# Stick-breaking attention in fixed turns, with odd blocks of tokens reversed and the running total in the last key's row

## The chip, the cores and the metric

One Trainium2 chip, one core of it. The metric is the device time of one execution in microseconds, median over runs. The core has a matrix engine (PE, TensorE), a vector engine (DVE, VectorE), a scalar engine (ACT, ScalarE), a general engine (POOL, GpSimd) and queues for transfers (SP). Each engine works through its own list of instructions in order; between engines, semaphores say when an operand is there or a buffer is free.

## The reference

Two decoder layers over 512 tokens of width 2048 in float32. The first is sparse attention with an indexer and a top-k; the second, which the change is about, is stick-breaking attention over keys and values that are computed once. Each layer ends with a gated output product, a layer norm and a gated per-layer embedding.

```python
def mixer_b(x, w_in, w_o, k, v):
    q, gate = jnp.split(x @ w_in, [WIDTH_B], axis=-1)      # 16 heads of 128, 4 key heads
    def block_fn(args):                                    # 128 queries at a time
        z = jnp.einsum('bqngd,bsnd->bngqs', qg, k).astype(jnp.float32) * (HEAD_DIM ** -0.5)
        strict = key_pos[None, :] < t[:, None]
        log_om = jnp.where(strict, -jax.nn.softplus(z), 0.0)
        suffix = lax.cumsum(log_om, axis=log_om.ndim - 1, reverse=True) - log_om
        a = jnp.where(strict, jnp.exp(jax.nn.log_sigmoid(z) + suffix), 0.0)
        o = jnp.einsum('bngqs,bsnd->bqngd', a.astype(v.dtype), v)
    return (o * jax.nn.silu(gate)) @ w_o
```

The weight of key s for query t is sigmoid(z) at s times the product of (1 - sigmoid(z)) over all keys between s and t. In logarithms that is z - (softplus(z) summed over the keys from s to t), so keys are worked through from the latest to the earliest and a total is carried from one block of keys to the next.

## The kernel before

Activations lie transposed, features in partitions and tokens along the free axis. All products are float32 made of three products of high and low parts: `split` (L131) copies the high part on ScalarE and subtracts on VectorE, `mm3` (L135) issues the three matmuls of 128x512. TensorE's order is exactly the order of the program text; the other engines' instructions are put in order by a scheduler, except for those that are held in program order (`paced`, L325, and `keep_in_program_order`).

The second layer's attention goes over four groups `g` of four heads, each with one key head. A group is worked together with the product for its gate: `gemm_w` (L289, and `gate_first`, L1213, for group 0) yields 64 steps, each of three matmuls, into four banks; every fourth step needs a new block of weights, which is split by one ScalarE and one VectorE instruction. `pumped` (L339) also does one piece of background work a step from the list `bg`: scaled and split queries of the next group (`split_scaled`, L1207), split keys, and in group 0 the restored halves of the layer's input (`restore`, L1147).

`sticks` (L1238) works the ten pairs of a query block i and a key block kb, `units` (L1240), in an order that alternates between query blocks. Four heads lie side by side, so each unit is 128 keys in partitions by 512. A unit has three parts:

- `logits` (L1245): three matmuls of keys and queries into a bank `z` (bank 7 for unit 0, then 4 and 5 in turn). On the diagonal (kb == i) VectorE adds the mask `gone`. ScalarE computes Abs, Exp and Ln; VectorE makes softplus out of them (L1258). Then comes bookkeeping in the first key's row, with instructions on one partition (L1259 to L1272): where a total is carried in, row 0 of `z` is replaced by the logarithm of sigmoid and row 0 of softplus by the total. At last VectorE splits softplus into `sh` and `sl`.
- `weights` (L1278): two matmuls with a triangle of -1 (`tri`, or `tri0` with a full first row, L1234) add the negative sums over the keys to `z` (L1282). VectorE takes the new total from row 0 (`y`, L1284); ScalarE computes Exp, and `split` makes high and low parts of the weights.
- `values` (L1292): three matmuls of values and weights into bank 6 or 7; after the last key block ScalarE copies the output into `F`.

The loop at L1300 issues `logits` of unit s, `weights` of s-1, `values` of s-2, for s from 0 to 11. `interleave` (L57) spreads the gate steps evenly between these parts: 64 - 18 over 28 parts in group 0 (L1343), 52 over 33 in the others after a lead of 8 (L1341), so some 1.6 gate steps behind each part. None of the instructions of `sticks` on ScalarE and VectorE is held in program order. After a group, four Silu and four multiplications apply the gate, and `log_exp` (L1222) loads the table of Exp and Ln again.

Of the kernel before, what the change touches and what calls it, by code (L numbers as in the profile page):

```python
# [10 lines left out]
F32 = mybir.dt.float32  # L11
# [7 lines left out]
T = 512  # L19
# [58 lines left out]
def trunk_kernel(  # L78
# [20 lines left out]
    class Paced:  # L99


        def __init__(self, engine):
            self.engine_ = engine
# [24 lines left out]
    def bank(i, name="ps"):  # L128
        return psum.tile([128, 512], F32, name=name, tag=f"bank{i}")

    def split(hi, lo, src, eng=dve):  # L131
        act.activation(hi, src, AF.Copy)
        eng.tensor_tensor(lo, src, hi.bitcast(F32), ALU.subtract)

    def mm3(out, a, b, start, stop):  # L135
        pe.matmul(out, a[0], b[0], start=start, stop=False)  # L136
        pe.matmul(out, a[0], b[1], start=False, stop=False)  # L137
        pe.matmul(out, a[1], b[0], start=False, stop=stop)  # L138
# [577 lines left out]
    def index_scores():  # L716
        for i in range(1, 4):
            w = 128 * (i + 1)
            for h in range(16):
                ps = spare("isc", 0)  # L720
                st = stacks[h][:, (i - 1) * 128 : i * 128]
                pe.matmul(ps[:, :w], st, B1[:, :w], start=True, stop=False)
                pe.matmul(ps[:, :w], st, B2[:, :w], start=False, stop=True)
                rl = ip.tile([128, T], F32, name="rl", tag="rl", bufs=3)
                act.activation(rl[:, :w], ps[:, :w], AF.Relu)
                wcol = iws[:, i - 1, h : h + 1]
                if h == 0:
# [5 lines left out]
            pool.affine_select(out=diag, in_=diag, pattern=[[-1, 128]], compare_op=ALU.is_ge, fill=FILL, base=0, channel_multiplier=1)  # L733
# [473 lines left out]
    def split_scaled(g, i):  # L1207
        qh, ql = (q.rearrange("p (h q) -> p h q", h=4) for q in Q[i])
        src = F[g][:, :, i * 128 : (i + 1) * 128]
        act.activation(qh, src, AF.Copy, scale=HSCALE)  # L1210
        dve.scalar_tensor_tensor(ql, src, HSCALE, qh.bitcast(F32), ALU.mult, ALU.subtract)
# [11 lines left out]
        tc.keep_in_program_order(act.preload_act_table_set("natural_log_exp_and_others"))  # L1223

    def work():
        return px.tile([128, 512], F32, name="wk", tag="wk", bufs=5)


    gone = px.tile([128, 128], F32, name="gone")
    pool.memset(gone, 0.0)  # L1230
    pool.affine_select(out=gone, in_=gone, pattern=[[1, 128]], compare_op=ALU.is_gt, fill=MASK, base=0, channel_multiplier=-1)
# [6 lines left out]
    def sticks(g, Q):  # L1238

        units = [(3, 3), (2, 2), (3, 2), (2, 1), (3, 1), (2, 0), (3, 0), (1, 1), (0, 0), (1, 0)]  # L1240
        total = {}
        state = {}
        out = {}

        def logits(u):  # L1245
            i, kb = units[u]
            z = bank(4 + u % 2 if u else 7, "z")
            ks = slice(kb * 128, (kb + 1) * 128)
            mm3(z, [k[:, ks] for k in K[g]], Q[i], True, True)
            e = work()  # L1250
            sp = work()
            if kb == i:
                v = z.rearrange("p (h q) -> p h q", h=4)
                dve.tensor_tensor(v, v, gone.unsqueeze(1).broadcast_to([128, 4, 128]), ALU.add)
            act.activation(e, z, AF.Abs)
            act.activation(e, e, AF.Exp, scale=-1.0)
            act.activation(e, e, AF.Ln, bias=1.0)
            dve.scalar_tensor_tensor(sp, z, 0.0, e, ALU.max, ALU.add)  # L1258
            first = None  # L1259
            if kb:  # L1260
                first = px.tile([1, 512], F32, name="y", tag="y", bufs=3)
            if kb == i:
                if kb:
                    dve.tensor_copy(first, z[0:1])
            else:

                if kb:
                    dve.scalar_tensor_tensor(first, z[0:1], 0.0, e[0:1], ALU.min, ALU.subtract)
                    dve.tensor_copy(z[0:1], first)
                else:  # L1270
                    dve.scalar_tensor_tensor(z[0:1], z[0:1], 0.0, e[0:1], ALU.min, ALU.subtract)
                dve.tensor_copy(sp[0:1], total.pop(i))  # L1272
            parts = tuple(px.tile([128, 512], F32R, name=f"s{s}", tag=f"s{s}", bufs=3) for s in "hl")
            dve.tensor_copy(parts[0], sp)
            dve.tensor_tensor(parts[1], sp, parts[0].bitcast(F32), ALU.subtract)
            state[u] = z, parts, first

        def weights(u):  # L1278
            i, kb = units[u]
            z, parts, first = state[u]  # L1280
            for n, p in enumerate(parts):
                pe.matmul(z, tri if kb == i else tri0, p, start=False, stop=n == 1, skip_group_check=True)  # L1282
            if kb:
                dve.tensor_tensor(first, first, z[0:1], ALU.subtract)  # L1284
                total[i] = first
            a = work()
            act.activation(a, z, AF.Exp)
            parts = A[u % 2]
            split(*parts, a)
            state[u] = parts  # L1290

        def values(u):  # L1292
            i, kb = units[u]
            if kb == i:
                out[i] = bank(6 if i in (0, 3) else 7, "o")
            mm3(out[i], [v[:, g * 128 : (g + 1) * 128] for v in V[kb]], state.pop(u), kb == i, kb == 0)
            if kb == 0:
                act.activation(F[g][:, :, i * 128 : (i + 1) * 128], out[i].rearrange("p (h q) -> p h q", h=4), AF.Copy)

        for s in range(12):  # L1300

            done = [i for n, (i, kb) in enumerate(units) if kb == 0 and s == max(n + 3, 0 if g else 8) and n < 9]
            if g < 3:
                bg.extend(lambda i=i: split_scaled(g + 1, i) for i in done)
            for fn, u in ((logits, s), (weights, s - 1), (values, s - 2)):
                if 0 <= u < 10:
                    fn(u)
                    yield
                if g and s == 1 and fn == logits:
                    for _ in range(4):  # L1310
                        yield

    log_exp()

# [5 lines left out]
    banks = mm_banks("g")  # L1320
    chunk = gate_first(banks)
    gemm = pumped(chunk)
    first = sticks(0, Q)
    for n in (9, 1):
        steps(gemm, n)
        steps(first, 1)
    bg.extend(lambda i=i: split_scaled(0, i) for i in (1, 0))
    steps(gemm, 8)
    gemm = pumped(chunk, 2)
# [1 line left out]
    for g in range(4):  # L1331
        if g:
            log_exp()
            banks = mm_banks("g")
            gemm = pumped(gemm_w(items, plain, banks))
        if 0 < g < 3:
            bg.append(lambda g=g: split_keys(g + 1))
        if g:
            sums = sticks(g, Q)
            steps(sums, 1)  # L1340
            interleave(sums, 29 + 4, gemm, 52, lead=8)  # L1341
        else:
# [60 lines left out]
```

## Time and profile before

| what | value |
|---|---|
| median of 3 runs | 1885.15 us (1885.1 to 1885.21) |
| profiled execution | 1884.75 us |
| its span, first to last instruction | 1882.9 us |
| granted TensorE clock | 1.000 |

Names: `z` is a bank of logits, `sh` and `sl` the parts of softplus, `y` the row with the total, `wk` any working tile, `wh` and `wl` the parts of a block of weights, `g` the banks of the gate, `o` those of an output (and of the next projection), `f` the tiles `F`, `c` the tiles with keys, values, queries and weights in parts. In the lists of groups, a row has the line, engine, operation, output and input, shape and count, then busy time, mean of one in nanoseconds, and the idle time in front of it with what ended it. A row of the timeline has the start, the duration, the engine and the instruction, and in brackets the idle time ahead of it. All of line 111 are ScalarE and VectorE instructions that were recorded through the class `Paced`. A row of waits says who waited for whom, microseconds in total, how often, and the longest.

### The profile page before, as it was taken

To read this page: it belongs to the slowest core of one execution; us is meant where nothing else is said; L and a number is where in the kernel's file an instruction comes from. 1 tells how busy PE (TensorE), PEld (TensorE's weight loads), DVE (VectorE), ACT (ScalarE), POOL (GpSimd) and SP (SyncE) were. 2 spreads that over 40 slices of the span, in tenths; PEclk is the share of its full clock that TensorE was granted. 3 is DMA by queue.
4 is the path that set the end of the run, shared out by engine and by line. 5 is a ranking of instruction groups with operands and counts; after the bars stand their busy time and mean duration, and the time that the engine had idled before them with its cause. 6 is when DMAs were issued, how large, how long until landed. Compare 5 with 4: busy or idle time off the path is not lost.

```text
span 1882.9 us, 24826 instructions
## 1 busy us (share of the span) xinstructions
PE 1860.2 (99%) x9181; PEld 1574.2 (84%) x9181; DVE 1247.3 (66%) x2444; ACT 923.5 (49%) x1672; POOL 3.9 (0%) x16
## 2 busy tenths in 40 slices
PE   9999999999999999999999999999999999999998
PEld 8898888888888888888888999977777788888887
DVE  5768678567565455675377888887887745567534
ACT  3546423455554432474245444467677643246422
POOL 0000000000000000000000000000000000000000
PEclk9999999999999999999999999999999999999999
DMA  6442333312222532433343333322121153242333
GB/s 196 127 124 62 96 101 90 101 56 68 72 65 66 180 99 77 125 101 113 105 144 110 105 100 109 104 78 89 56 68 57 56 190 95 79 129 91 123 101 112
DMA packets 111179, 189.21 MB, mean 100 GB/s; under 512 B 8529, under 2 KB 29009, under 8 KB 111057
## 3 DMA queue, kind: packets, MB, share of 16 engines
q1 hardware_dynamic: 111056, 187.62, 32.7%
q8 instruction: 72, 1.18, 0.3%
q14 instruction: 51, 0.41, 0.1%
HBM read 179.21 MB, written 8.39 MB: 100 GB/s over the span
## 4 chain that ended last, share of the span: by engine, by line
PE 93%; DVE 3%; ACT 2%; issue 1%; DMA 0%; SPq 0%; DVEq 0%; ACTq 0%
PE g L136 11%; PE g L137 11%; PE g L138 11%; PE o L137 7%; PE o L136 7%; PE o L138 7%; PE m L136 4%; PE m L138 4%; PE m L137 4%; PE q L137 3%; PE q L138 3%; PE q L136 3%; PE k L137 2%; PE k L138 2%; PE k L136 2%; ACT wk L111 1%
## 5 line engine op out<-in xcount | busy, mean ns | idle before, releaser
L111 ACT ACTIVATE wh<-raw 128x512 fp32r<-128x512 f32 (+3 forms) x685 | 397.8, 582 | 703.7 <-PE g L137 235.2
L111 DVE TENSOR_TENSOR wl<-raw,wh 128x512 fp32r<-128x512 f32 (+3 forms) x685 | 430.3, 629 | 460.4 <-ACT wh L111 443.0
L136 PE MATMUL g<-xh,wh 128*128 128x512 f32 x1024 | 403.9, 394 | 0.0
L138 PE MATMUL g<-xh,wl 128*128 128x512 f32 x1024 | 399.5, 390 | 0.0
L137 PE MATMUL g<-xl,wh 128*128 128x512 f32 x1024 | 399.5, 390 | 0.0
L138 PEld LDWEIGHTS g<-xh,wl 128*128 128x128 f32 x1024 | 192.2, 188 | 41.2
L136 PEld LDWEIGHTS g<-xh,wh 128*128 128x128 f32 x1024 | 192.4, 188 | 37.6 <-ACT wk L111 0.8
L137 PEld LDWEIGHTS g<-xl,wh 128*128 128x128 f32 x1024 | 192.5, 188 | 37.2
L138 PE MATMUL o<-xh,wl 128*128 128x512 f32 x512 | 199.2, 389 | 0.0
L136 PE MATMUL o<-xh,wh 128*128 128x512 f32 x512 | 199.2, 389 | 0.0
L137 PE MATMUL o<-xl,wh 128*128 128x512 f32 x512 | 199.2, 389 | 0.0
L138 PEld LDWEIGHTS o<-xh,wl 128*128 128x128 f32 x512 | 96.1, 188 | 20.2
L136 PEld LDWEIGHTS o<-xh,wh 128*128 128x128 f32 x512 | 96.1, 188 | 19.9
L137 PEld LDWEIGHTS o<-xl,wh 128*128 128x128 f32 x512 | 96.1, 188 | 19.8
L136 PE MATMUL q<-xh,wh 128*128 128x512 f32 x256 | 99.6, 389 | 0.0
L137 PE MATMUL q<-xl,wh 128*128 128x512 f32 x256 | 99.6, 389 | 0.0
L138 PE MATMUL q<-xh,wl 128*128 128x512 f32 x256 | 99.6, 389 | 0.0
L111 ACT ACTIVATE wk<-z 128x512 f32<-128x512 f32 x80 | 47.4, 594 | 58.5 <-DVE z L111 24.2
L111 ACT ACTIVATE sh<-st 128x512 fp32r<-128x512 f32 x80 | 49.7, 624 | 44.4 <-DVE st L111 44.3
L111 DVE TENSOR_TENSOR sl<-st,sh 128x512 fp32r<-128x512 f32 x80 | 55.2, 691 | 13.9 <-ACT sh L111 13.9
L111 DVE TENSOR_TENSOR xl<-f,xh 128x512 fp32r<-128x512 f32 x80 | 54.3, 686 | 12.6 <-ACT f L111 12.3
L136 PEld LDWEIGHTS q<-xh,wh 128*128 128x128 f32 x256 | 48.0, 188 | 10.1
(284 smaller groups left out, 3327.0 us busy)
## 6 DMA issues: line engine op xcount, KB each, us to landing
raw<-w_in_a SPq DMA_DIRECT2D x95, 512.0 KB, 3.7
raw<-w_in_b SPq DMA_DIRECT2D x64, 512.0 KB, 3.8
raw<-w_ple_gate SPq DMA_DIRECT2D x52, 512.0 KB, 3.7
raw<-w_o_a SPq DMA_DIRECT2D x24, 512.0 KB, 3.8
raw<-w_o_b SPq DMA_DIRECT2D x24, 512.0 KB, 3.8
raw<-w_kv_b SPq DMA_DIRECT2D x16, 512.0 KB, 3.8
raw<-w_ple_gate SPq DMA_DIRECT2D x24, 256.0 KB, 2.9
f<-xT SPq DMA_DIRECT2D x4, 1024.0 KB, 6.3
```

The source lines that it names most:

```text
L111: ins = method(*args, **kw)
L136: pe.matmul(out, a[0], b[0], start=start, stop=False)
L137: pe.matmul(out, a[0], b[1], start=False, stop=False)
L138: pe.matmul(out, a[1], b[0], start=False, stop=stop)
```

## The change

- Odd query and key blocks (1 and 3) hold their 128 tokens in descending order. The host reorders the columns of x, of the embeddings and of the positions, and the rows of the result. The masks of the diagonal blocks are flipped for odd blocks, and a second triangle, `down`, serves odd key blocks.
- With that the total that is carried from one key block to the next lies in the last key's row: partition 0 for even key blocks, partition 127 for odd ones (instructions there work on the 32 rows from 96, with a column of the identity as factor so that only row 127 counts). The total is added to that row of softplus ahead of its split, so row 0 of `z` is no longer replaced. A copy of that row of `z` is taken on ScalarE ahead of the sums, and VectorE subtracts the new row from it afterwards.
- The splitting of softplus becomes a part of its own, `parts`. In `weights`, Exp is issued ahead of the subtraction for the total.
- `Sticks.turn` fixes the order: `logits` of s, gate steps, `values` of s-2, gate steps, `weights` of s-1 and `parts` of s, gate steps. The gate steps are 1, 1 and 3 in an ordinary turn (2 at the end of odd turns in group 0). Units 0 and 1 begin ahead of the turns; in groups 1 to 3, 11 gate steps follow them.
- All of these parts are called through `paced`, so their ScalarE and VectorE instructions are held in program order. The gate's weight splits and the Silu part are not.
- Buffers: `wk` 6 for 5, parts of softplus 2 for 3.

```diff
-    tri0 = px.tile([128, 128], F32R, name="tri0")
-    dve.tensor_copy(tri0, tri.bitcast(F32))
-    dve.tensor_copy(tri0[0:1], neg[0:1].bitcast(F32))
+    down = px.tile([128, 128], F32R, name="down")
+    gone = [px.tile([128, 128], F32, name=f"gone{n}") for n in range(2)]
...
+    for m, up in zip(gone, (1, -1)):
+        pool.memset(m, 0.0)
+        pool.affine_select(out=m, in_=m, pattern=[[up, 128]], compare_op=ALU.is_gt, fill=MASK, base=0, channel_multiplier=-up)
...
             act.activation(e, e, AF.Ln, bias=1.0)
             dve.scalar_tensor_tensor(sp, z, 0.0, e, ALU.max, ALU.add)
-            first = None
...
-                    dve.scalar_tensor_tensor(first, z[0:1], 0.0, e[0:1], ALU.min, ALU.subtract)
-                    dve.tensor_copy(z[0:1], first)
...
-                dve.tensor_copy(sp[0:1], total.pop(i))
...
+        def parts(self, u):
...
+            if kb < i:
+                total = self.total.pop(i)
+                if kb % 2:
+                    dve.tensor_tensor(sp[0:1], sp[0:1], total[0:1], ALU.add)
+                else:
+                    rows = slice(96, 128)
+                    dve.scalar_tensor_tensor(sp[rows], total[rows], ident[rows, 127:128], sp[rows], ALU.mult, ALU.add)
+            hi, lo = (px.tile([128, 512], F32R, name=f"s{s}", tag=f"s{s}", bufs=2) for s in "hl")
+            dve.tensor_copy(hi, sp)
+            dve.tensor_tensor(lo, sp, hi.bitcast(F32), ALU.subtract)
             if kb:
+                rows = slice(96, 128) if kb % 2 else slice(0, 1)
+                self.total[i, kb] = px.tile([128, 512], F32, name="t", tag="t", bufs=3)
+                act.activation(self.total[i, kb][rows], z[rows], AF.Copy)
...
+            for n, p in enumerate((hi, lo)):
+                pe.matmul(z, down if kb % 2 else tri, p, start=False, stop=n == 1, skip_group_check=True)
             a = work()
             act.activation(a, z, AF.Exp)
+            if kb:
+                rows = slice(96, 128) if kb % 2 else slice(0, 1)
+                total = self.total[i] = self.total.pop((i, kb))
+                dve.tensor_tensor(total[rows], total[rows], z[rows], ALU.subtract)
+            hi, lo = A[u % 2]
+            split(hi, lo, a)
...
+            pe.matmul(o, vh, hi, start=kb == i, stop=False)
+            pe.matmul(o, vl, hi, start=False, stop=False)
+            pe.matmul(o, vh, lo, start=False, stop=kb == 0)
...
+        def begin(self, u):
+            paced(self.logits, u)
+            if u == 0:
+                paced(self.parts, u)
+
+        def turn(self, s, gemm, gaps):
+            if 1 < s < 10:
+                paced(self.logits, s)
+            steps(gemm, gaps[0])
+            if s > 1:
+                paced(self.values, s - 2)
+            steps(gemm, gaps[1])
+            if s < 11:
+                paced(self.weights, s - 1)
+                if s < 10:
+                    paced(self.parts, s)
+            steps(gemm, gaps[2])
+            if self.g < 3 and s > 6:
+                bg.extend(lambda i=i: split_scaled(self.g + 1, i) for i in {8: (2,), 9: (3,), 11: (0,)}.get(s, ()))
...
-            interleave(sums, 29 + 4, gemm, 52, lead=8)
-        else:
-            interleave(first, 30 - 2, gemm, 64 - 18)
+        steps(gemm, 11 if g else 0)
+        for s in range(1, 12):
+            sticks.turn(s, gemm, (0 if s == 1 else 1, 1 if s > 1 else 0, 2 if s == 10 or not g and s % 2 else 3))
+        run(gemm)
...
-        "xT": lay(np.asarray(x)[0].T),
+        "xT": lay(np.asarray(x)[0][order].T),
```

More of the change, by code (lines that the diff above doesn't have):

```diff
@@ L1225, in work, with __init__, logits @@
     def work():
[L1226 to L1231, printed above, removed]
-    tri0 = px.tile([128, 128], F32R, name="tri0")
-    dve.tensor_copy(tri0, tri.bitcast(F32))
-    dve.tensor_copy(tri0[0:1], neg[0:1].bitcast(F32))
-    def sticks(g, Q):
-        units = [(3, 3), (2, 2), (3, 2), (2, 1), (3, 1), (2, 0), (3, 0), (1, 1), (0, 0), (1, 0)]
[L1241 to L1246, printed above, removed]
+        return px.tile([128, 512], F32, name="wk", tag="wk", bufs=6)
+    down = px.tile([128, 128], F32R, name="down")
+    gone = [px.tile([128, 128], F32, name=f"gone{n}") for n in range(2)]
+    ones = work()[:, :128]
+    pool.memset(ones, -1.0)
+    pool.affine_select(out=ones, in_=ones, pattern=[[1, 128]], compare_op=ALU.is_ge, fill=0.0, base=0, channel_multiplier=-1)
+    dve.tensor_copy(down, ones)
+    for m, up in zip(gone, (1, -1)):
+        pool.memset(m, 0.0)
+        pool.affine_select(out=m, in_=m, pattern=[[up, 128]], compare_op=ALU.is_gt, fill=MASK, base=0, channel_multiplier=-up)
+    class Sticks:
+        units = [(3, 3), (2, 2), (3, 2), (2, 1), (3, 1), (2, 0), (3, 0), (1, 1), (0, 0), (1, 0)]
+        def __init__(self, g):
+            self.g = g
+            self.total = {}
+            self.state = {}
+            self.out = {}
+        def logits(self, u):
+            i, kb = self.units[u]
             z = bank(4 + u % 2 if u else 7, "z")
             ks = slice(kb * 128, (kb + 1) * 128)
-            mm3(z, [k[:, ks] for k in K[g]], Q[i], True, True)
+            mm3(z, [k[:, ks] for k in K[self.g]], Q[i], True, True)
             e = work()
@@ L1253, in logits @@
                 v = z.rearrange("p (h q) -> p h q", h=4)
-                dve.tensor_tensor(v, v, gone.unsqueeze(1).broadcast_to([128, 4, 128]), ALU.add)
+                dve.tensor_tensor(v, v, gone[i % 2].unsqueeze(1).broadcast_to([128, 4, 128]), ALU.add)
             act.activation(e, z, AF.Abs)
@@ L1273, in logits @@
[L1273 to L1285, printed above, removed]
+            self.state[u] = z, sp
@@ L1286, in weights @@
+        def weights(self, u):
+            i, kb = self.units[u]
+            z, hi, lo = self.state[u]
+            for n, p in enumerate((hi, lo)):
+                pe.matmul(z, down if kb % 2 else tri, p, start=False, stop=n == 1, skip_group_check=True)
             a = work()
             act.activation(a, z, AF.Exp)
[L1288 to L1293, printed above, removed]
-            if kb == i:
-                out[i] = bank(6 if i in (0, 3) else 7, "o")
-            mm3(out[i], [v[:, g * 128 : (g + 1) * 128] for v in V[kb]], state.pop(u), kb == i, kb == 0)
-            if kb == 0:
-                act.activation(F[g][:, :, i * 128 : (i + 1) * 128], out[i].rearrange("p (h q) -> p h q", h=4), AF.Copy)
@@ L1300, in sticks @@
[L1300 to L1311, printed above, removed]
+            if kb:
+                rows = slice(96, 128) if kb % 2 else slice(0, 1)
+                total = self.total[i] = self.total.pop((i, kb))
+                dve.tensor_tensor(total[rows], total[rows], z[rows], ALU.subtract)
@@ new lines, in weights, with values @@
+            hi, lo = A[u % 2]
+            split(hi, lo, a)
+            self.state[u] = hi, lo
+        def values(self, u):
+            i, kb = self.units[u]
+            if kb == i:
+                self.out[i] = bank(6 if i in (0, 3) else 7, "o")
+            o = self.out[i]
+            hi, lo = self.state.pop(u)
+            vh, vl = (v[:, self.g * 128 : (self.g + 1) * 128] for v in V[kb])
+            pe.matmul(o, vh, hi, start=kb == i, stop=False)
+            pe.matmul(o, vl, hi, start=False, stop=False)
+            pe.matmul(o, vh, lo, start=False, stop=kb == 0)
+            if kb == 0:
+                act.activation(F[self.g][:, :, i * 128 : (i + 1) * 128], o.rearrange("p (h q) -> p h q", h=4), AF.Copy)
@@ L1322, in trunk_kernel @@
     gemm = pumped(chunk)
[L1323 to L1326, printed above, removed]
+    sticks = Sticks(0)
+    steps(gemm, 9)
+    sticks.begin(0)
+    steps(gemm, 1)
+    sticks.begin(1)
     bg.extend(lambda i=i: split_scaled(0, i) for i in (1, 0))
@@ L1379 @@
     ln = np.stack([np.asarray(ln_g), np.asarray(ln_b)]).reshape(2, 2, NK, 128)
+    order = np.arange(T).reshape(4, 128)
+    order[1::2] = order[1::2, ::-1].copy()
+    order = order.ravel()
+    lay = np.ascontiguousarray
+    ln = np.stack([np.asarray(ln_g), np.asarray(ln_b)]).reshape(2, 2, NK, 128)
     ins = {
-        "xT": lay(np.asarray(x)[0].T),
-        "pT": lay(np.asarray(p)[:, 0].transpose(0, 2, 1)),
-        "pos": lay(np.asarray(positions)),
+        "xT": lay(np.asarray(x)[0][order].T),
+        "pT": lay(np.asarray(p)[:, 0][:, order].transpose(0, 2, 1)),
+        "pos": lay(np.asarray(positions)[:, order]),
         "rope_c": rope,
@@ L1401 @@
     r = _run(nc, [ins], core_ids=[0])
-    return lay(np.asarray(r.results[0]["out_0_dram"]).T)[None]
+    return lay(np.asarray(r.results[0]["out_0_dram"]).T[order])[None]
```

20 lines of the change are left out of this document (8 added, 12 removed).

## The prediction

> **What bounds the kernel now.** I read the page first, then who makes TensorE wait, then the stretch with the stick-breaking layer row by row.
>
> ```profile
> span 1882.9 us, 24826 instructions
> PE 1860.2 (99%) x9181; PEld 1574.2 (84%) x9181; DVE 1247.3 (66%) x2444; ACT 923.5 (49%) x1672; POOL 3.9 (0%) x16
> PE 93%; DVE 3%; ACT 2%; issue 1%; DMA 0%; SPq 0%; DVEq 0%; ACTq 0%
> ```
>
> TensorE sets the time almost everywhere; only what makes it wait can be gained or lost. The list of TensorE's waits has nearly everything in one place, the banks `z` of the stick-breaking layer:
>
> ```profile
> PE z L1282 <- DVE sl L111: 7.1, 13, 1.3
> PE z L136 <- ACT wk L111: 4.5, 6, 1.0
> PE z L1282 <- DVE sh L111: 3.1, 7, 0.6
> ...
> PE o L137 <- DVE c L111: 1.2, 1, 1.2
> ```
>
> Line 1282 is the sum over the keys (`weights`), line 136 the first product of `logits`, line 137 a product of `values`. These microseconds undercount, because a matmul counts as busy for its 0.39 us although the next starts sooner. From the timeline of TensorE:
>
> ```profile
> 1342.77 0.39 PE L138 MATMUL o<-c,c 128*128 128x512 f32 x1
> ...
> 1345.94 0.47 PE L1282 MATMUL z<-sl,tri 128*128 128x512 f32 x1
> ...
> 1361.46 0.39 PE L138 MATMUL g<-xh,wl 128*128 128x512 f32 x1
> 1362.49 0.50 PE L1282 MATMUL z<-sh,tri 128*128 128x512 f32 x1 [0.64 <-DVE sh L111]
> 1363.22 0.50 PE L1282 MATMUL z<-sl,tri 128*128 128x512 f32 x1 [0.22 <-DVE sl L111]
> 1363.55 0.40 PE L136 MATMUL g<-xh,wh 128*128 128x512 f32 x1
> ```
>
> Fourteen undisturbed intervals lie between the first two rows: 3.17 / 14 = 0.2264 us a matmul. The pair at 1362.49 takes 2.09 us where three intervals are 0.68: 1.41 lost, of which the view names 0.86. So I count by pace. The layer's matmuls run from the first gate product to the first of the next projection:
>
> ```profile
> L136 PE MATMUL o<-c,c x40: 387/389/395, 1251.6 to 1501.9; 128*128 128x512 f32 x40
> L136 PE MATMUL o<-xh,wh x20: 389/389/389, 1506.6 to 1519.5; 128*128 128x512 f32 x20
> L136 PE MATMUL g<-xh,wh x256: 389/389/499, 1233.4 to 1505.9; 128*128 128x512 f32 x128
> ```
>
> That is 3 x 256 gate products, 3 x 40 values, 3 x 40 logits and 2 x 40 sums, 1088 in 1506.6 - 1233.4 = 273.2 us. At 0.2264 they need 246.3. **26.9 us of stall** is all that this change can win (61.6 us a group of four heads is the floor, 68.3 is used). Going through the starts, about 16.5 of it stands before `weights`, 7 before `logits`, 1.5 before `values`. The rest is small.
>
> **The change part by part.** TensorE's work stays: 1088 matmuls, only `values` orders its three so that the low part of the weights comes last (0.23 us more slack for it). What moves is the work around it. Rows by kind, in this stretch:
>
> ```profile
> L111 DVE SCALAR_TENSOR_TENSOR wk<-z,wk 128x512 f32<-128x512 f32 x40 | 27.4, 685 | 13.5 <-ACT wk L111 13.5
> L111 DVE TENSOR_TENSOR sl<-wk,sh 128x512 fp32r<-128x512 f32 x40 | 27.3, 682 | 0.4
> ...
> L111 DVE TENSOR_TENSOR y<-y,z 1x512 f32<-1x512 f32 x24 | 16.1, 671 | 3.8 <-PE z L1282 3.8
> ...
> L111 DVE COPY wk<-y 1x512 f32<-1x512 f32 x24 | 9.7, 405 | 0.0
> ...
> L111 DVE SCALAR_TENSOR_TENSOR z<-z,wk 1x512 f32<-1x512 f32 x12 | 8.2, 685 | 0.3
> L111 DVE COPY z<-y 1x512 f32<-1x512 f32 x12 | 8.1, 675 | 0.0
> L111 DVE SCALAR_TENSOR_TENSOR y<-z,wk 1x512 f32<-1x512 f32 x12 | 8.0, 669 | 0.0
> L111 DVE COPY y<-z 1x512 f32<-1x512 f32 x12 | 8.0, 669 | 0.0
> ...
> L111 ACT ACTIVATE wk<-wk 128x512 f32<-128x512 f32 x80 | 50.1, 627 | 1.6
> L111 ACT ACTIVATE wk<-z 128x512 f32<-128x512 f32 x80 | 47.4, 594 | 58.5 <-DVE z L111 24.2 <-PE z L138 12.4 <-DVE y L111 11.5
> ```
>
> *First-row bookkeeping.* A one-row instruction costs what a full one does (671 against 682 ns). The four kinds on `y` and `z` and the copy `wk<-y` go: 9.7 + 8.2 + 8.1 + 8.0 + 8.0 = 42.0 us. One addition for each of 24 later blocks comes; 24 x 0.68 = 16.3. VectorE loses 25.7 us, 6.4 a group. The copy of the last row out of `z` moves to ScalarE, 24 x 0.594 = 14.3 us, 3.6 a group. Neither row is for 32 rows; both neighbours (1 and 128 rows) agree within 2%, so no range is needed.
>
> ```profile
> sum 273.17, PE 256.96 PEld 201.77 DVE 219.67 ACT 190.82 POOL 0.50; mean PE 64.24 PEld 50.44 DVE 54.92 ACT 47.70 POOL 0.13
> ```
>
> From these means over the four groups, VectorE goes to 48.5 and ScalarE to 51.3 of the 61.6 us: neither becomes the bound by its sum.
>
> *The fixed turns.* Times below count from the first logits product of a turn in groups 1 to 3 (3 logits, 3 gate, 3 values, 3 gate, 2 sums, 9 gate = 23 matmuls, 5.21 us). The rows that set steps and latencies:
>
> ```profile
> 1344.25 0.41 DVE L111 CAST sh<-wk 128x512 fp32r<-128x512 f32 x1
> ...
> 1344.58 0.67 DVE L111 TENSOR_TENSOR wl<-raw,wh 128x512 fp32r<-128x512 f32 x1
> ...
> 1345.18 0.67 DVE L111 TENSOR_TENSOR sl<-wk,sh 128x512 fp32r<-128x512 f32 x1
> ...
> 1345.79 0.68 DVE L111 TENSOR_TENSOR z<-z,gone 128x512 f32<-128x512 f32 x1
> ...
> 1346.50 0.60 ACT L111 ACTIVATE wk<-z 128x512 f32<-128x512 f32 x1 [2.22 <-DVE z L111]
> ...
> 1347.67 0.62 ACT L111 ACTIVATE wh<-raw 128x512 fp32r<-128x512 f32 x1
> ...
> 1348.19 0.61 ACT L111 ACTIVATE wk<-wk 128x512 f32<-128x512 f32 x1
> ...
> 1348.71 0.57 ACT L111 ACTIVATE f<-o 128x512 f32<-128x512 f32 x1
> ...
> 1349.19 0.59 ACT L111 ACTIVATE wk<-z 128x512 f32<-128x512 f32 x1
> ...
> 1349.83 0.50 PE L136 MATMUL z<-c,c 128*128 128x512 f32 x1 [0.68 <-ACT wk L111]
> ...
> 1356.91 0.40 PE L138 MATMUL z<-c 128*128 128x512 f32 x1
> ...
> 1357.34 0.60 ACT L111 ACTIVATE wk<-z 128x512 f32<-128x512 f32 x1 [0.39 <-PE z L138]
> ```
>
> VectorE steps on by 0.61 us (0.33 after a copy between tiles), ScalarE by 0.52 between independent instructions and 0.63 between dependent ones; a product is seen 0.43 after its start. An ordinary turn s: Abs 0.88, Exp 1.51, Ln 2.14, end 2.77; softplus on VectorE 2.80. Sums of s-1 at 2.72 and 2.94, Exp 3.37, high part 4.00 to 4.63, VectorE's subtraction from the total 4.00 to 4.67, low part 4.66, addition of the total 5.27, `sh` 5.88, `sl` 6.21 to 6.9. The sums of s need `sl` at 5.21 + 2.94 = 8.15: **slack 1.2 us** on the chain that makes up 16.5 us of today's stall. The gate split of each fourth gate step (one instruction on either engine, 1.25 a turn) fits in it. So the waits before `weights` go, but for what the diagonal units cause.
>
> *The diagonal units 7 and 8.* Their mask stands in VectorE's fixed order behind `sl` of the unit before, which lets the engine go at 6.82 - 5.21 = 1.61. Mask to 2.3, Abs 2.3, Ln done 4.2, copy of a finished output 0.52, perhaps one gate split 0.52, and only then Exp of unit 6: 4.7 or 5.2, done 5.3 or 5.8. Logits of unit 8 want that bank at 5.21: 0.1 to 0.6 late, I take 0.5. One turn on the same chain starts later: `sl` of unit 7 is done near 2.3 of turn 8, Exp of unit 7 ends at 6.0 to 6.5. Then the subtraction for its total reads the same bank. Today ScalarE waits 11.5 us for that subtraction (`DVE y`), so the two readers go one behind the other; in the new order Exp is first, the subtraction second, and the bank is free at 6.7 to 7.2: 1.5 to 2.0 late for logits of unit 9, I take 1.8. Today's stalls at these places (the 0.68 at 1349.83 and its next) cost about 2.2 a group, so here nothing is won.
>
> The Trainium skill, "PSUM — Partial Sum Buffer", section "PSUM bank collisions raise a hardware error", states that two engines must not be in one bank and the same 32 partitions at once, two readers included. The trace agrees, by the 11.5 us above. Without that rule the subtraction would run beside Exp and unit 9 would be 0.8 to 1.3 late; the sum below would be some 3 us better.
>
> *Group 0* has a gate step less in odd turns (4.53 us). The subtraction ends at 4.67 and later, with a restore or a split in front up to 0.9 late: 0.35 in each of four turns, 1.4. Unit 8 then 5.7 - 4.53 = 1.2, unit 9 1.8; its start, crowded by restored halves and scaled queries, 0.7; the last sums 0.3. Together 5.4.
>
> *At no cost:* six mask instructions on POOL for two, the flipped selections in the first layer (same number and size), the reversed input rows (same bytes). POOL is otherwise idle; at its mean of 3.9 / 16 = 0.24 us the first mask could wait six times that, 1.5 us, once, if POOL got its buffer late.
>
> **Sum.** Groups 1 to 3: 0.5 + 1.8 + 0.3 for the last sums + 0.5 for a split in a bad place at the start of a group = 3.1 each (1.6 to 5 by the bounds), 9.3. With group 0, 14.7 stay of 26.9: **12.2 us won**. The profiled execution took 1884.75 us, 1.85 around its span; 1872.6 by this sum, and the median of the runs is 0.4 above it: **1873**.
>
> **Rivals.** *All hidden.* The pieces between Abs and Exp fall elsewhere, since the gate splits are not held in order. Then about 1 us a group stays: 26.9 - 4 = 22.9 won, 1862. For it: VectorE gets 6.4 us a group back. Against: the mask's place is fixed. *Stalls only move.* As the change lets go of 25.7 us that VectorE does not lack by its sum (54.9 of 68.3 busy), the waits turn up at the bank's release: 0.6 in each of 36 turns is 21.6, gain 5 or less, 1880 to 1883. *The fixed order makes a convoy; slower.* Place: ScalarE's queue between Abs of unit s and Exp of unit s-1. Each restored half, output copy, scaled query or split there (0.52) delays Exp, and VectorE's low part, addition and parts stand behind it. Slack at the bank is 5.21 - 4.67 = 0.54 after ScalarE's idle 0.6; four pieces (2.08) leave each turn 0.94 late, 36 x 0.94 = 34 us against 26.9: 1892. It decides from 26.9 / 36 = 0.75 a turn. Against: a turn has 1.25 splits and about one other piece, not four.
>
> **How the numbers follow.** Forecast 0.45 (1867 to 1878 by its bounds), all hidden 0.25, moved 0.15 (half of it gains over 3.8 us), convoy 0.15. A run set tells 0.2%, 3.8 us, from no change. Faster 0.45 + 0.25 + 0.08 = 0.78, same 0.07, slower 0.15. The range 1862 to 1888 leaves out the convoy's bulk and the best of the hidden case.
>
> **What would show it.** Right: waits of line 1282 for `sl` and `sh` fall from 10.2 to under 3; `logits` of units 8 and 9 still wait, the latter for a VectorE subtraction; VectorE's busy time falls by about 26 us, ScalarE's rises by 14. Wrong: waits in every turn, on `sl` or on the bank (moved, convoy), or a gap in front of the first mask.

## The result and the profile after

| | before | changed |
|---|---|---|
| median of 13 runs each, side by side | 1885.1 us | 1888.66 us |
| lowest and highest | 1884.74 to 1885.51 | 1888.13 to 1890.2 |
| profiled execution, span | 1884.75, 1882.9 us | 1889.72, 1888.0 us |

The ratio is 1.0021, 95% interval 1.0013 to 1.003: 3.6 us slower, where 12 us faster was forecast. The range's upper end was 1888.

The page of the changed kernel, lines that answer to those of before:

```profile
span 1888.0 us, 24839 instructions
PE 1865.0 (99%) x9181; PEld 1577.3 (84%) x9181; DVE 1235.1 (65%) x2395; ACT 938.6 (50%) x1696; POOL 4.7 (0%) x20
```

As many matmuls, 49 VectorE instructions less, 24 ScalarE instructions more. VectorE's busy time falls by 12.2 us, ScalarE's rises by 15.1. Who made TensorE wait in the changed kernel (microseconds in total, times, longest; line 1291 is now the sums, 1310 to 1312 the values):

```profile
PE z L136 <- DVE t L111: 9.0, 5, 2.5
PE o L1310 <- ACT c L111: 2.6, 4, 1.0
PE z L1291 <- DVE sl L111: 2.5, 8, 0.7
PE z L1291 <- DVE sh L111: 1.5, 2, 1.1
...
PE o L1312 <- DVE c L111: 0.5, 1, 0.5
```

The waits of the sums on the parts of softplus fell from 10.2 to 4.0 us, as forecast in kind. In their place stand 9.0 us in which logits wait for VectorE's subtraction into `t`, nearly all of it in front of unit 9. By pace, as in the prediction, between the same first and last products:

```profile
L136 PE MATMUL g<-xh,wh x256: 387/389/628, 1234.0 to 1511.0; 128*128 128x512 f32 x128
```

```profile
L136 PE MATMUL o<-xh,wh x27: 389/389/389, 1511.7 to 1529.4; 128*128 128x512 f32 x27
```

1511.7 - 1234.0 = 277.7 us for the same 1088 matmuls, 31.4 above 246.3; before it was 26.9. Part of this is no wait. The row of the gate has a longest matmul of 628 ns, where before it was 499. Windows of one microsecond in group 0 show why (columns: window, its length, busy time and count of PE, PEld, DVE, ACT, POOL, then the granted TensorE clock, the transfers' share and GB/s):

```profile
1253.00:1254.00 1.00, 0.54 (x2) 0.43 (x3) 0.97 (x3) 0.94 (x3) 0.00 (x0) 0.86 0.82 176
1254.00:1255.00 1.00, 1.00 (x4) 0.81 (x3) 0.97 (x2) 0.41 (x1) 0.00 (x0) 0.50 0.97 343
...
1257.00:1258.00 1.00, 1.00 (x6) 0.82 (x5) 1.00 (x2) 1.00 (x3) 0.00 (x0) 0.94 0.00 0
```

After two waits of 1.0 and 0.5 us the granted clock stands at 0.50 for some three and a half microseconds, and matmuls start 0.43 us apart and not 0.2264. Three windows of 10 us have a mean clock of 0.83 in this execution, at 1250, 1290 and 1490; the other two follow the wait at unit 9. Each loses 10 x 0.17 = 1.7 us, together 5.1. In the profile of before no such window is found. So the waits proper are 31.4 - 5.1 = **26.3 us, against 26.9 before**: they moved, and the clock is the loss. The 13 times of the changed kernel lie in two clusters, 1888.13 to 1888.66 and 1889.72 to 1890.2, with middles 1.5 apart. That is near the 1.7 of one spell; that one spell more makes the difference is argued from this size, since only one execution was profiled.

Where a spell begins follows a grid. In this trace the granted clock changes only at whole multiples of 3.413 us: the spells last 3.413 each, the stretches between them 37.55 and 197.97 us, which is 11 and 58 times that. Cut on this grid, the stretch ahead of the spell at 1294.67 is nearly empty, while the wait in front of unit 9 in group 1, at 1360, is split between two stretches (PE alone: busy time and count, with matmuls that still run from the stretch before; then the clock, the transfers' share and GB/s):

```profile
1291.26:1294.67 3.41, 0.90 (x4) 1.00 0.29 63
1294.67:1298.09 3.42, 3.42 (x10) 0.50 0.23 90
...
1359.53:1362.94 3.41, 2.00 (x9) 1.00 0.00 0
```

Over the traces of all 14 kernels, 13 spells begin while TensorE still has work. In the stretch of the grid before each of them it started 6 matmuls or fewer, where 15 fit. Two other stretches had 6 and no spell behind them, one of them at the wait of group 2; none with 7 or more had one.

Where the wait in front of unit 9 comes from (timeline of group 1, turn 8; products of the gate left out):

```profile
1355.11 0.69 DVE L111 TENSOR_TENSOR wl<-raw,wh 128x512 fp32r<-128x512 f32 x1 [0.25 <-ACT wh L111]
...
1355.72 0.68 DVE L111 TENSOR_TENSOR sl<-wk,sh 128x512 fp32r<-128x512 f32 x1
...
1356.33 0.69 DVE L111 TENSOR_TENSOR z<-z,gone 128x512 f32<-128x512 f32 x1
...
1356.64 0.39 PE L1291 MATMUL z<-sl,down 128*128 128x512 f32 x1
...
1357.05 0.60 ACT L111 ACTIVATE wk<-z 128x512 f32<-128x512 f32 x1 [0.53 <-DVE z L111]
...
1358.22 0.62 ACT L111 ACTIVATE wh<-raw 128x512 fp32r<-128x512 f32 x1
1358.69 0.39 PE L138 MATMUL g<-xh,wl 128*128 128x512 f32 x1
1358.74 0.61 ACT L111 ACTIVATE wk<-wk 128x512 f32<-128x512 f32 x1
...
1359.26 0.58 ACT L111 ACTIVATE wk<-z 128x512 f32<-128x512 f32 x1
1359.48 0.68 DVE L111 SCALAR_TENSOR_TENSOR wk<-z,wk 128x512 f32<-128x512 f32 x1
...
1360.19 0.69 DVE L111 TENSOR_TENSOR t<-t,z 32x512 f32<-32x512 f32 x1
...
1360.94 0.50 PE L136 MATMUL z<-c 128*128 128x512 f32 x1 [1.87 <-DVE t L111]
```

The mask of unit 8 waits in VectorE's list behind a gate split and `sl` of unit 7; Abs of unit 8 follows it; Exp of unit 7, whose sums were started by 1356.64, stands in ScalarE's list behind Abs, Exp, a gate split and Ln of unit 8 and runs at 1359.26. The subtraction comes after that, but not at once: softplus of unit 8 (1359.48) is held ahead of it in VectorE's list, so it starts 0.35 us after Exp has ended. In turns 2 to 5 of groups 1 to 3 it starts 0.03 us after Exp's end. TensorE's last gate product was started at 1358.69 and the next logits at 1360.94.

### The profile page after: what moved, and what is told of

The parts are those of the page before. It is cut to its first block, busy times and chain, and to the rows that moved or that the text cites. A ratio compares the mean times of both kernels' runs of the same rounds, so it can differ in the third digit from the quotient of the medians.

```text
span 1888.0 us, 24839 instructions
## 1 busy us (share of the span) xinstructions
PE 1865.0 (99%) x9181; PEld 1577.3 (84%) x9181; DVE 1235.1 (65%) x2395; ACT 938.6 (50%) x1696; POOL 4.7 (0%) x20
## 4 chain that ended last, share of the span: by engine, by line
PE 94%; DVE 3%; ACT 2%; issue 1%; DMA 0%; SPq 0%; ACTq 0%; DVEq 0%
PE g L136 11%; PE g L137 11%; PE g L138 11%; PE o L138 7%; PE o L136 7%; PE o L137 7%; PE m L136 4%; PE m L138 4%; PE m L137 4%; PE q L136 3%; PE q L138 3%; PE q L137 3%; PE k L137 2%; PE k L138 2%; PE k L136 2%; ACT wk L111 1%
## 5 line engine op out<-in xcount | busy, mean ns | idle before, releaser
L138 PEld LDWEIGHTS q<-xh,wl 128*128 128x128 f32 x256 | 48.0, 188 | 10.1
```

## The experiments

All times are medians with the kernel before run beside them (1884.45 to 1884.63 in these sets, four runs or more of each kernel). The changed kernel was not run again in these sets, so a difference to its 1888.66 is good to some 0.6 us, by which the kernel before stands lower here than beside it. "Stall" is the excess over 0.2264 us a matmul in the same stretch, clock spells included.

| kernel | time | against before | stall |
|---|---|---|---|
| before | 1885.1 | | 26.9 |
| changed | 1888.66 | 1.0021 (1.0013 to 1.003) | 31.4 |
| x1 changed, order free | 1878.56 | 0.9967 (0.9955 to 0.998) | 20.5 |
| x2 changed, no mask on units 7, 8 | 1874.94 | 0.9949 (0.9937 to 0.9962) | 16.6 |
| x3 changed, stall filled | 1885.46 | 1.0005 (0.9996 to 1.0014) | 18.7 |
| x4 changed, gate steps moved | 1886.33 | 1.0009 (1.0 to 1.0018) | 26.7 |
| x5 changed, mask by TensorE | **1870.92** | 0.9928 (0.9916 to 0.9941) | 9.3 |
| x6 as x5, order free | 1873.22 | 0.9939 (0.9926 to 0.9953) | 11.6 |
| x7 bookkeeping alone | 1882.45 | 0.999 (0.9982 to 0.9999) | 24.2 |
| x8 before, order held | 1930.63 | 1.0245 (1.0231 to 1.0259) | 73.4 |
| x9 as x5, VectorE's load put back | 1871.53 | 0.993 (0.9917 to 0.9944) | 9.7 |
| x10 before, mask by TensorE | 1880.74 | 0.9979 (0.997 to 0.9988) | 19.1 |
| x11 as x5, gate steps moved | 1871.83 | 0.9932 (0.992 to 0.9945) | 10.0 |
| x13 changed, no subtraction of unit 7 | 1877.92 | 0.9966 (0.9954 to 0.9978) | 20.9 |

### x1: the order set free

```diff
-                paced(self.logits, s)
+                self.logits(s)
...
-                paced(self.weights, s - 1)
+                self.weights(s - 1)
-                    paced(self.parts, s)
+                    self.parts(s)
```

> TensorE's order of the changed kernel is kept; ScalarE's and VectorE's instructions of the sticks are no longer held in program order. Theory 'fixed order' (Exp of unit 7 is held behind Ln of unit 8, which waits for its mask): the wait in front of unit 9 falls from 2.0 us to under 1.0 in groups 1 to 3, and the time to 1878 to 1884. Rival 'spacing' (the gate steps stand wrongly, whatever the engines' order): the wait stays at 1.5 or more and the time at 1887 to 1890.

The time came as expected, the reason did not. Waits of TensorE with a free order:

```profile
PE z L136 <- DVE t L111: 8.4, 9, 1.7
PE o L1312 <- DVE c L111: 3.6, 5, 1.1
```

Logits still wait for the subtraction, 1.72 us at unit 9 in groups 1 to 3. What went are the waits of the sums on `sh` and `sl` (4.0 us in the changed kernel), those of `values` on ScalarE at the start of a group (2.6) and the clock spells. So the scheduler's order is worth 10.1 us to the changed kernel, but unit 9's wait is not a matter of holding alone: in the free order too the mask of unit 8 stands behind `sl` of unit 7 (it starts at 1348.56 in group 1) and Exp of unit 7 behind Ln of unit 8 (1352.30).

### x2: two masks left out

```diff
-            if kb == i:
+            if kb == i and u not in (7, 8):
```

> Leaves out the addition of the mask on units 7 and 8 (the diagonal blocks of queries 1 and 0), so their weights are not causal. Theory 'fixed order': Abs starts 0.9 us after the logits, Exp of unit 7 near 3.4 of its turn, and the wait in front of unit 9 (2.0 to 2.7 in each group) goes; 4 x 2.2 = 9 us less, and half of the half-clock spells with it (1.7 us each), so 1876 to 1880. Rival 'spacing': over 1 us of that wait stays and the time is over 1884.

1.1 us below the range given. Of the waits on the subtraction one in group 0 is left; those for `sl`, `sh` and `c` stay nearly as they were:

```profile
PE o L1310 <- ACT c L111: 2.6, 4, 1.0
PE z L1291 <- DVE sl L111: 2.1, 8, 0.6
PE z L1291 <- DVE sh L111: 1.5, 2, 1.1
...
PE z L136 <- DVE t L111: 0.8, 1, 0.8
```

The two masks in the chain cost 13.7 us by the medians and 14.8 between the profiled executions. By pace 8.8 us of the latter stood in front of unit 9 (2.70 in group 0, 2.03 in each other), 5.1 were the clock spells, of which this execution has none, and some 0.6 another wait in group 0. One of the three spells, in group 0's start, followed waits that are still there with this edit (1.20 and 0.71 us by pace); that it is missing here is luck and not the edit's work.

### x3: the same wait, filled with work

```diff
+            if s == 9:
+                idle = bank(6, "spin")
+                for n in range(9):
+                    pe.matmul(idle, tri, Q[3][0], start=n == 0, stop=n == 8)
```

> Adds nine matmuls of 128x512 (2.04 us) into the free bank 6 in front of the logits of unit 9 in each group; nothing reads them. They lie in the wait that is there already. If the half clock comes from TensorE's idle time, the spells behind unit 9 go and only the one in group 0's start stays: 1884.5 to 1887, granted clock 0.999. If the clock falls for another reason, it stays at 0.997 and the time at 1888 to 1890.

36 matmuls more, and 3.2 us faster. The wait for the subtraction shrinks from 9.0 to 1.3 us, since TensorE is busy during it:

```profile
PE z L136 <- DVE t L111: 1.3, 2, 0.8
```

36 x 0.2264 = 8.15 us of new work lie in it, and 18.7 + 8.15 = 26.9 is near the changed kernel's 26.3. Nothing about the chain changed; only TensorE did not stand still. The granted clock of the whole execution is 0.999 (0.997 in the changed kernel), and no window of 10 us in the layer is below 0.995. The half clock is thus a consequence of the wait and cost some 3 us in the median. Runs from 1884.66 to 1887.19 suggest that a spell still occurs in some; one wait, in group 0's start, was not filled.

### x4: gate steps in front of unit 9

Turns 3, 4 and 5 end with 2 gate steps for 3, turn 8 with 6 for 3, in groups 1 to 3.

> In groups 1 to 3 turns 3, 4 and 5 give up one gate step each and turn 8 ends with six instead of three, so 2.04 us more work stands in front of unit 9. Theory 'fixed order' with slack in ordinary turns: the wait of 2.03 goes in three groups, no new wait in turns 3 to 6; 6 us and one half-clock spell less, 1880 to 1883. If ordinary turns have no slack, the wait turns up in turns 4 to 6 and the time is 1886 or more.

A miss: 1886.33, which is in the range of the other case. The profiled execution took 1884.73 and has no clock spell. The waits in it:

```profile
PE z L136 <- DVE t L111: 3.4, 2, 2.5
...
PE z L136 <- ACT wk L111: 2.5, 3, 0.8
```

Unit 9 no longer waits in groups 1 to 3, but unit 8 now does, 0.82 us in each, as turn 7 is reached earlier against the same chain; and three turns lose 0.2 each at their logits, so the slack of ordinary turns is below the 0.68 that was taken. By pace all waits add up to 26.7 us, against 26.3 in the changed kernel: they moved. Cover at the last link of a late chain did not mend it here.

### x5: the mask added by TensorE

```diff
+            if kb == i:
+                pe.matmul(v, ident_r, gone_r[i % 2].unsqueeze(1).broadcast_to([128, 4, 128]), start=True, stop=False)
+            mm3(z, keys, Q[i], kb != i, True)
...
-                dve.tensor_tensor(v, v, gone[i % 2].unsqueeze(1).broadcast_to([128, 4, 128]), ALU.add)
```

> The changed kernel, its order held, with the mask of the diagonal units added by TensorE (one more matmul of the identity and the mask in each of 16 diagonal units, 16 x 0.2264 = 3.6 us) and not by VectorE. Theory 'mask link' (VectorE's place for the mask, behind the parts of the unit before, starts the chain that is late at unit 9 and in a group's start): the wait in front of unit 9 goes in all groups and most of the 1.7 us in each group's start; from the 1874.9 without two masks, 3.6 more and 4 x 1.5 less: 1870 to 1875. Rival (the lateness comes from the length of ScalarE's list): unit 9 still waits over 1 us and the time is 1882 or more.

1870.92, 17.7 below the changed kernel and 13.7 below the kernel before, though TensorE has 3.6 us more work. What is left:

```profile
PE z L1297 <- DVE sl L111: 1.1, 5, 0.3
PE z L1297 <- DVE sh L111: 1.1, 1, 1.1
PE z L136 <- DVE t L111: 0.8, 1, 0.8
PE z L1264 <- DVE goner L111: 0.7, 1, 0.7
```

The same part of group 1 as above, units 8 and 9 (only rows on `z` and `t` shown):

```profile
1345.09 0.39 PE L1264 MATMUL z<-goner,identr 128*128 128x512 f32 x1
...
1345.77 0.39 PE L138 MATMUL z<-c,c 128*128 128x512 f32 x1
1346.19 0.60 ACT L111 ACTIVATE wk<-z 128x512 f32<-128x512 f32 x1 [0.23 <-PE z L138]
...
1348.69 0.60 ACT L111 ACTIVATE wk<-z 128x512 f32<-128x512 f32 x1
...
1349.42 0.69 DVE L111 TENSOR_TENSOR t<-t,z 32x512 f32<-32x512 f32 x1
...
1350.53 0.39 PE L136 MATMUL z<-c 128*128 128x512 f32 x1
```

Abs of unit 8 starts 0.42 us after its last product and not 2.91 (1357.05 - 1354.14 in the changed kernel, whose third product started at 1354.14); the subtraction of unit 7 is done at 1350.11, ahead of the logits that need the bank.

### x6: x5 with a free order

> As x5, and the sticks' instructions not held in program order. If what the held order costs (10.1 us between the changed kernel and x1) and what the mask link costs are two things, they add: 1864 to 1870. If both are the same microseconds, it comes out as the better of x1 and x5.

The effects do not add: 1873.22, 2.3 us behind x5, a miss (1872.86 to 1873.44 against 1870.59 to 1871.65). Holding the order, which cost the changed kernel 10.1 us, gains 2.3 once the mask is out of VectorE's list. `values` wait for VectorE's low part in the free order (2.8 us in five waits), which the held order had ahead.

### x7: the bookkeeping alone

Last-row totals, reversed blocks and Exp ahead of the subtraction, in the loop and with the spread of gate steps of the kernel before, order free.

> Only the bookkeeping of the change (last-row totals, reversed odd blocks, Exp ahead of the subtraction); order of parts, spread of the gate steps and freedom of the scheduler as before. Theory 'the saved VectorE work is real, the turns and the held order lose it': 1876 to 1881. Rival 'VectorE's saved work was hidden anyway': 1883 to 1886.

Between the two ranges and nearer the rival's: 1882.45, 2.1 us won, with 25.7 us less of VectorE's work by the prediction's count. Waits of the sums fall from 10.2 to 7.0 us, those of logits rise:

```profile
PE z L136 <- DVE t L111: 6.5, 4, 2.3
PE z L1291 <- DVE sl L111: 6.4, 12, 1.1
```

So the wait for the subtraction comes with the bookkeeping, which puts it behind Exp. It is there in old turns and free order as well.

### x8: the kernel before with its order held

```diff
-                    fn(u)
+                    paced(fn, u)
```

> The kernel before with one edit: logits, weights and values are held in program order on ScalarE and VectorE. If holding is a cost of its own, as x1 suggests, the time rises by 6 to 15 us (1891 to 1900), with waits in front of the sums and of logits in many turns. If it only hurts in the new turns, 1884 to 1887.

46 us, three times what was expected at most. TensorE waits for ScalarE in front of logits:

```profile
PE z L136 <- ACT wk L111: 40.5, 18, 5.0
```

and twelve windows of 10 us have a clock below 0.995. TensorE ran at one half for 34.1 us in the layer, which makes 17.1 of the 73.4 us of stall; the waits proper are some 56. A likely reason lies in the text of the kernel: in the old spread, Exp of a unit is written behind Abs, Exp and Ln of the next, whose products come just ahead of its sums. The scheduler had mended that; the held order takes the text at its word.

### x9: chain or load

x5, and in each diagonal unit VectorE adds the mask, spread to 128x512, to itself into a scratch tile at the place where the mask was added (0.68 us each, the mask 0.70); ScalarE does not wait for it.

> As x5 (mask added by TensorE), and VectorE does an addition of the same size (128x512 into a scratch tile that nothing reads) at the place in its held order where the mask stood, so its load is that of the changed kernel, but ScalarE's Abs does not wait for it. Theory 'link': the time stays within 3 us of x5, 1871 to 1874. Rival 'load' (x5 is faster because VectorE has 16 instructions, 11 us, less): at least half of the 17.7 us comes back, 1880 or more.

1871.53, 0.6 above x5. The mask's 11 us on VectorE are worth little; its place between the products and Abs is worth some 17, the clock spells included.

### x10: the kernel before with the mask on TensorE

> The kernel before with the mask of the diagonal units added by TensorE and nothing else changed. If the mask's link is what the kernel before loses too, the waits of logits on ScalarE (4.5 us) and some of those on VectorE's parts go: 1876 to 1881. If the mask only hurts in the held turns, 1884 to 1889 (3.6 us of matmuls added).

1880.74, 3.9 better than before, 0.2% with an interval clear of 1. The waits of logits on ScalarE (4.5 us) are gone, those of the sums are not:

```profile
PE z L1286 <- DVE sl L111: 6.6, 13, 0.9
PE z L1286 <- DVE sh L111: 3.2, 7, 0.7
```

The turns of the changed kernel remove most of the sums' waits (x1), the mask on TensorE those of the logits; x5 has both.

### x11: gate steps in x5

One gate step from the lead (in group 0 from turn 2) to the end of turn 9.

> As x5, with one gate step moved in front of the last sums: in groups 1 to 3 from the lead to the end of turn 9, in group 0 from turn 2 to turn 9. The waits of the last units' sums (0.9 in two groups, 0.36 in one, 1.8 in group 0) shrink by up to 0.68 each: 1868 to 1870. If the lead or turn 2 was needed, as much comes back there and it stays at 1871.

1871.83, no gain. The last sums wait 0.4 instead of 0.7 in groups 1 and 2, and as much comes back at the values of unit 0 and in group 0's early turns. x5 is the best version here.

### x13: the second reader of the bank

```diff
+                if u != 7:
+                    dve.tensor_tensor(total[rows], total[rows], z[rows], ALU.subtract)
...
+                if u == 9:
+                    pass
```

> The changed kernel without VectorE's subtraction for the total of unit 7 and without the addition of that total in unit 9, in all four groups, so unit 9 carries no total. Theory of the prediction ('two readers, one behind the other'): the bank is free at the end of Exp of unit 7 and not after the subtraction, so the wait in front of unit 9 falls from 2.0 to about 1.0 in groups 1 to 3, and the half clock behind it becomes rare: 1881 to 1885. Rival (the subtraction runs beside Exp, or only Exp counts): the wait stays at 1.8 or more, 1887 to 1889.

The wait at unit 9 is 0.82 us in groups 1 to 3 instead of 1.87, and now for ScalarE:

```profile
PE z L136 <- ACT wk L111: 4.0, 4, 1.5
```

So the subtraction behind Exp costs 1.05 us at that place, its own 0.69 and the 0.35 that it starts after Exp's end. The latter comes from softplus of unit 8 ahead of it in VectorE's list, so this does not show what the subtraction would cost if it ran beside Exp. The time fell further than expected, to 1877.92: the addition in unit 9 went as well, and with it most of the wait of unit 9's sums (3.6 us by pace in the four groups, 0.8 left); there is one clock spell in this execution and not three.

## Why the prediction was wrong, point by point

**The floor and the bookkeeping.** 26.9 us of stall was the right ceiling: x5 used 17.6 of it. VectorE's saving was sized at 25.7 us of busy time; the page shows 12.2. The term was mis-sized, in the rows by kind of the layer:

```profile
L111 DVE SCALAR_TENSOR_TENSOR wk<-t,ident,wk 32x512 f32<-32x512 f32 x16 | 12.0, 751 | 0.5
...
L111 DVE TENSOR_TENSOR t<-t,z 32x512 f32<-32x512 f32 x16 | 11.1, 693 | 3.4 <-ACT wk L111 3.1
...
L111 DVE TENSOR_TENSOR wk<-wk,t 1x512 f32<-1x512 f32 x8 | 5.4, 672 | 0.0
```

The addition costs 12.0 + 5.4 = 17.4 us and not 16.3, so rows of 42.0 - 17.4 = 24.6 us went; other rows grew, and all VectorE rows together fell by 22.0. But rows overlap, since an instruction of 0.68 us steps on after 0.61, and the page counts time in which at least one runs: where VectorE is less crowded, each row counts in full. It did not matter: x9 shows that VectorE's load is not the bound, as the prediction said of its sum.

**Ordinary turns: right in groups 1 to 3.** From the third turn to the last gate product before unit 9 they have next to no stall (0.16 us by pace from 1326.15 to 1358.69 in group 1, 0.2 in groups 2 and 3). The sums' wait fell to 4.0 us, forecast under 3.

**Units 8 and 9: right in mechanism, near in size.** Unit 9 waits for the subtraction, 2.0 us by pace in groups 1 to 3 where 1.8 was taken; unit 8 not at all where 0.5 was taken. x2, x5 and x9 show that the mask's place starts it, x13 that the subtraction costs 1.05 of it. One step of the reason was off: the subtraction was said to start late because Exp reads the same bank, and in the ordinary turns it does start 0.03 us behind Exp, but at unit 9 softplus of unit 8 in VectorE's list ends 0.32 us after Exp and sets its start. The Trainium skill, "PSUM — Partial Sum Buffer", section "PSUM bank collisions raise a hardware error", has it that two engines must not read a bank and the same 32 partitions at once. The 0.03 us of the ordinary turns agree with that; no run here tests it at unit 9.

**The start and the end of a group: mis-sized.** The term "0.5 for a split in a bad place at the start of a group" measured 1.7, 1.9 and 2.7 in groups 1 to 3, by pace up to the third turn. It is the mask again, of unit 1: x2, which keeps that mask, keeps these waits, and x5 has almost none of them. Rows of the changed kernel's group 2 from ScalarE, VectorE and TensorE:

```profile
1385.60 0.69 DVE L111 TENSOR_TENSOR z<-z,gone 128x512 f32<-128x512 f32 x1
...
1386.33 0.60 ACT L111 ACTIVATE wk<-z 128x512 f32<-128x512 f32 x1 [1.68 <-DVE z L111]
...
1388.53 1.07 ACT L111 ACTIVATE wk<-z 128x512 f32<-128x512 f32 x2
...
1389.49 0.63 ACT L111 ACTIVATE c<-wk 128x512 fp32r<-128x512 f32 x1
...
1390.17 0.50 PE L1310 MATMUL o<-c,c 128*128 128x512 f32 x1 [0.54 <-ACT c L111]
```

ScalarE stands idle 1.68 us for the mask, which waits behind `sl` of unit 0 (from 1384.99), and Exp of unit 0 is held behind Ln of unit 1. The prediction followed this chain for units 7 and 8 and not for unit 1. The last sums wait 0.7 in groups 1 and 2 and 0.4 in group 3, where 0.3 was taken; x5 has the same waits, so they are not the mask's.

**Group 0: mis-sized.** 5.4 us were forecast. Its excess is 13.7, of which 3.4 are two clock spells: 10.3. Its start has 2.4 (0.7 taken), of which 1.9 in front of `values` of unit 0; the turns between start and unit 9 have 3.2 (1.4 taken, and 1.2 for unit 8), unit 9 has 2.7 (1.8 taken), its last sums 1.8 (0.3 taken).

**The clock: missing.** The sum had no term for it. 5.1 us in the profiled execution, some 3 in the median by x3. The Trainium skill, "TensorE: Matmul & The Clock Gate", section "Part 1: The HAM clock gate (the "warmup" mystery)", has it that the clock goes to one half when TensorE has been idle over a window of about 3.4 us, and comes back after a busy one. The trace agrees on the half (0.50) and on the length of a spell (3.413 us). But TensorE was not idle for a whole stretch of that length: waits of 1.9 and 2.5 us, or of 1.0 and 0.5 close together, were enough where they left 6 started matmuls or fewer in one stretch of the grid, and two of 1.9 us, at 1360 and 1427, left the clock alone.

**The verdict on the rivals.** By the total, what happened is "stalls only move" (26.9 to 26.3), given 0.15, with the clock on top; but they do not stand in every turn, as that rival had it. Their place, ScalarE's list between Abs of one unit and Exp of the unit before, is the convoy's, but at the masks alone and not in each turn.

The step that failed is the sum of what stays. 14.7 us were taken; waits of 26.3 were measured, 16.0 in groups 1 to 3 (9.3 taken) and 10.3 in group 0 (5.4 taken), and 5.1 of half clock, for which the sum had no term. x5 leaves 9.3 us, so 17.0 of the 26.3 hang on the mask's place ahead of Abs. The prediction counted that place at units 7 and 8 and not at the start of a group. Holding the order adds to it, but x1 shows that unit 9 waits 1.7 us in the free order too. What keeps the other 9.3 us, above all the last sums and the turns of group 0, was not taken apart.

## What to carry to other kernels

When an order is fixed by hand, look for the one instruction whose operand comes late, and count everything that stands behind it on both engines; sixteen masks took 11 us of VectorE, which were nearly free, and their place cost some 17 us. Where the matrix engine is the bound, one more matmul of 0.23 us can be the cheapest place for a small step that otherwise crosses two engines. A wait of two microseconds on TensorE can cost nearly twice its length (1.9 and 1.7 for the clock), so a few waits of one microsecond, far apart, may be cheaper than one long one; that was not tried by itself.

## What the runs showed of the hardware

TensorE's clock was granted at one half after waits of some 2 us, for 3.413 us, which cost 1.7 us each; not after each such wait. Filling most of the wait with matmuls that nothing reads made the kernel 3.2 us faster. Whether a wait is followed by the half clock goes with how it lies to a grid of 3.413 us: 6 matmuls or fewer were started in the stretch before each of 13 spells, while stretches with 7 or more had no spell behind them. Two stretches with 6 had none either, so the exact limit stays open. An instruction of VectorE on 32 rows with a column as factor took 751 ns, where the same kind on 128 rows and without took 691; that was not tried by itself.
